# MLP entry of a two-layer hybrid step: twelve early weight pairs, earlier first splits, later squares and low parts

## The chip, the cores and the metric

The kernel runs on one core of one Trainium2 chip. The metric is device time in microseconds (us), here the median of three runs. The core has a matrix engine (PE), whose weight loads are a row of their own (PEld), a vector engine (DVE), a scalar engine (ACT), GpSimd (POOL), and a queue on SyncE (SP) that issues all DMA transfers in order.

## The reference, cut to what matters

Two layers. Each normalises the 1152 tokens (1024 latent, 128 prompt), runs three parallel groups (convolution, grouped attention, neighbourhood attention), adds their output projection, and then runs the MLP:

```
x = x + g1 * (concat(a_out, b_out, c_out) @ w_out)
h = rms(x, n2) * (1 + sc2) + sh2
x = x + g2 * (square(relu(h @ w1)) @ w2)
```

`w1` is 1024 x 4096, all in float32. The change touches only the step from the output projection through `h @ w1`.

## The kernel before

**Precision.** Each float32 product is made of three matmul passes (`three`, L1315): high part times high part, high times low, low times high. Each operand is split: ACT casts the high part (`w1h`, `HA`, `hi`), DVE subtracts it to get the low part (`w1l`, `low`). DVE works in the order written, ACT too; all orders are written by hand.

**Seven products for eight.** `h @ w1` goes by a Strassen-Winograd scheme over two halves of the model dimension, two halves of the tokens (576 each; T half 0 and 1), and pairs of weight columns. There are 16 pairs `g`; each needs seven products P1 to P7 (table `PRODUCTS`). One product is 24 matmuls of 288 columns. P1 and P2 need only the blocks B11 and B21, that is `h` of token half 0. The other five need sums in which half 1 takes part (blocks T1 to T4, B22).

**Early pairs.** So P1 and P2 of the first `EARLY` pairs are computed while the normalised half 1 is still being made. Their P1 result is stored to DRAM (`sd`) and read back (`again`) when the pair's other five products come; the weights A11 and A12 are loaded a second time with the pair's four blocks. I call this stretch the entry: it begins when PE ends the output projection (tile `pso`) and ends with the first P6 (tile `psb`). After it come five products for each early pair and seven for each later (late) pair.

**What runs in the entry.** The loop at L1665 goes over `seq`: three P1, then P2 and P1 in turn, three P2 at the end (`LEAD` 3). At each product it loads one weight block (`load_next`) and splits one (`begin_next`) that PE uses three products later; it computes the product (`psa` for P1, `psd` for P2) and takes the result out (`taken`: ACT copies P1 into `ev`; DVE adds P2 to it, and ACT then applies relu and square, `squared`). Then `next(pre)` runs one step of `norm2(L, 1)`: three steps of 1/rms, then per block index a step A that scales and shifts `X` (DVE, then ACT) and a step B that forms the sums of the halves (five DVE instructions and one ACT cast), then eight steps that cast the blocks and write their low parts (`low`). An extra step runs after every fourth product. A low part is held back by one call (`late`), so that DVE does not wait for the ACT cast just issued.

**Before the entry.** `out_proj` (L1321) makes eight output parts for each token half. During the last four parts of half 1 it runs `norm2(L, 0)` for half 0, and after each of them one step of `M.begin()`, whose eight steps are five loads and then three splits; the four steps left run behind the last part.

**After the entry.** For the late pairs of layer 0 every fourth product runs one step of `modulation(1, [0])` (`fill`): eight of its steps load four blocks `aw` of 256 KB each and do four matmuls. PSUM banks (`P`, eight) and the tiles of the shared pools S (18 of 2 x 576, among them `X`, `ev`, `low`) and T (18, among them all weight tiles) are given in turn.

Of the kernel before, what the change touches and what calls it, by code (L numbers as in the profile page):

```python
# [28 lines left out]
SEGS = [(0, 512), (512, 512), (1024, 128), (1024, 64), (1088, 64)]  # L29
HT, HH = 576, 288  # L30
ARENA = 229344 - 64 * NT
EARLY, LEAD = 8, 3
POOL_TAPS = 22
GPOOL = 6
SCAN = 12
# [10 lines left out]
def hybrid_step(ctx, tc, I, O, depth=DEPTH):  # L46
# [77 lines left out]
    sd = [dram.tile([EARLY, 128, 2 * HT], F32, name=f"sd{l}") for l in range(depth)]  # L124
    hd = [dram.tile([7, 16, 128, HT], F32, name=f"hd{l}") for l in range(depth)]
# [1195 lines left out]
    def out_proj(L, op, M):  # L1321
        l = L.l
        g1 = mod[l][:, :, 16:24]
        norms = {si: Norm(si, (nc.vector, nc.vector)) for si in (0, 3, 1, 4)}
        w, late = op.w, []

        def keep():
            while late:
                n, t = late.pop(0)
                load(dy[l][:, n, t * HT:(t + 1) * HT], X[n][:, t, :])  # L1330

        def part(n, t):
            ps = [P("pso"), P("pso")]
            for k in range(KT):
                three(ps, w[n][0][:, k, :], w[n][1][:, k, :], c_block(0, k, t), c_block(1, k, t), k == 0, k == KT - 1)
                yield "begun"
            update(ps, X[n][:, t, :], g1, n)
            norms[t].add(n)
            norms[3 + t].add(n)
            keep()  # L1340
            late.append((n, t))
            if t:
                w.pop(n)

        for n in range(KT):
            op.prep(n)
            if n == 0:
                yield from part(n, 0)
            op.prep(n + 1)
            if n:  # L1350
                run(part(n, 0))
            op.fetch()
            if n < 4:
                run(part(n, 1))
        keep()
        g0 = norm2(L, 0, norms)
        begin = M.begin()
        for n in range(4, KT):
            for k, _ in enumerate(part(n, 1)):
                if k in (1, 4, 6):  # L1360
                    next(g0, None)
            next(begin, None)
        run(begin)
        run(g0)
        yield "rest"
        for i, _ in enumerate(norm2(L, 1, norms)):
            if i == 2:
                keep()
            yield
# [18 lines left out]
    def norm2(L, t, norms):  # L1388

        l = L.l  # L1390
        gs = [norms[si].rstd() for si in (t, 3 + t)]
        for _ in range(3):
            for g in gs:
                next(g, None)
            yield

        def modulated(k):
            for s, si in enumerate((t, 3 + t)):
                x = xs(k, si)
                stt(x, x, A2[l][:, s, k:k + 1], norms[si].rstd_all, ALU.mult, ALU.mult)  # L1400
            for s, si in enumerate((t, 3 + t)):
                x = xs(k, si)
                act(x, x, ACTF.Identity, bias=mod[l][:, s, 24 + k:25 + k])

        late = []

        def parts(b, i, src):

            hi, lo = block(L, b, i)
            acopy(hi, src)  # L1410
            if late:
                late.pop()()
            late.append(partial(tt, lo, src, f32(hi), ALU.subtract))

        if t == 0:
            for i in range(4):
                for b, k in (("B11", i), ("B21", 4 + i)):
                    modulated(k)
                    parts(b, i, X[k][:, 0, :])
                    yield  # L1420
            late.pop()()
            return
        L.hi34 = {b: [S([2, HT], F32R, n="hi34") for _ in range(2)] for b in ("T3", "T4")}
        modulated(0)
        modulated(4)
        for i in range(4):
            if i < 3:
                modulated(i + 1)
                modulated(5 + i)
                yield  # L1430
            x1, x2, y1, y2 = X[i][:, 0, :], X[i][:, 1, :], X[4 + i][:, 0, :], X[4 + i][:, 1, :]
            raw = ha(10, i, HF)
            tt(x1, x2, x1, ALU.subtract)
            tt(raw, y2, x1, ALU.subtract)
            parts("T2", i, raw)
            tt(x2, y2, x2, ALU.subtract)
            tt(y1, y1, raw, ALU.subtract)
            yield
        L.low = {}
        for k in range(KT):  # L1440
            L.low[k] = S([2, HT], F32R, n="low")
            for u, b in enumerate(("T1", "T3") if k < 4 else ("T4", "B22")):
                parts(b, k % 4, X[k][:, u, :])
            yield
        late.pop()()


    class Mlp:
# [57 lines left out]
    def mlp(L, M, pre, fill, last):  # L1506
        l = L.l
        g2 = mod[l][:, :, 40:48]
        banks, ev, stores = {}, {}, []

        def keep(n=0):
            while len(stores) > n:
                load(*stores.pop(0))
# [90 lines left out]
        def squared(x):  # L1604
            act(x, x, ACTF.Relu)
            act(x, x, ACTF.Square)

        def taken(g, p, ps):
            early = g < EARLY
            if p == "P1":  # L1610
                ev[g] = [S([2, HT], n="ev")]
            if p == "P6":
                ev[g].append(S([2, HT], n="ev"))
            e1 = ev[g][0]
            e2 = ev[g][1] if len(ev[g]) > 1 else e1
            s1, h11 = e1[:, 0, :], e1[:, 1 if early else 0, :]
            u2, u3 = (e2[:, 0, :], e2[:, 1, :]) if early else (e1[:, 1, :], e2[:, 0, :])
            h21 = s1 if early else e2[:, 1, :]
            for h in range(2):
                c = slice(h * HH, (h + 1) * HH)  # L1620
                x = ps[h][:, 0:HH]
                to = {"P1": s1, "P2": h11, "P6": u2, "P5": u3, "P7": u3, "P3": u2, "P4": h21}[p][:, c]
                if p in ("P1", "P5") or p == "P6" and not early:
                    acopy(to, x)
                elif p == "P4" and not early:
                    act(to, x, ACTF.Relu)
                    tt(to, x, to, ALU.mult)
                else:
                    tt(to, x, (s1[:, c] if p in ("P2", "P6") else to), ALU.add)
            if p == "P2":  # L1630
                squared(h11)
                if early:
                    stores.append((sd[l][g], e1.rearrange("p a c -> p (a c)")))
                stores.append((hd[l][0, g], h11))
                if early:
                    del ev[g]
            elif p == "P7":
                if early:
                    tt(u3, u3, s1, ALU.add)
                squared(u3)  # L1640
                stores.append((hd[l][2, g], u3))
            elif p == "P3":
                squared(u2)
            elif p == "P4":
                if early:
                    squared(h21)
                stores.append((hd[l][1, g], h21))
                e3, e4 = S([2, HT], n="ev"), S([2, HT], n="ev")
                for b, o, x, y in ((3, e3[:, 0, :], u2, h11), (4, e3[:, 1, :], u3, e3[:, 0, :]),
                                   (5, e4[:, 0, :], u3, u2), (6, e4[:, 1, :], h21, e3[:, 1, :])):  # L1650
                    tt(o, x, y, ALU.subtract)
                    stores.append((hd[l][b, g], o))
                del ev[g]
# [10 lines left out]
            seq += [(g, "P2")] + [(g + LEAD, "P1")] * (g + LEAD < EARLY)  # L1664
        for x, (g, p) in enumerate(seq):  # L1665
            M.begin_next()
            product(g, p)
            keep(2)
            next(pre, None)
            if x % 4 == 3:  # L1670
                next(pre, None)
            if x == len(seq) - 6:
                M.load1(0, ("A11", "A21", "A22", "A12"))
            if x == len(seq) - 2:
                M.sums1(0)
        keep()
        again(0)
        seq = [(g, p) for g in range(EARLY) for p in ("P6", "P5", "P7", "P3", "P4")]
# [18 lines left out]
        for x, (g, p) in enumerate(seq):  # L1697
            if p == "P5" and g + 1 < NG:
                M.load1(g + 1, ("A11", "A21", "A22", "A12"))
            if p == "P7" and g + 1 < EARLY:  # L1700
                again(g + 1)
            prepare(x + 1)
            prepare(x + 2)
            product(g, p)
            keep(3)
            if g >= EARLY and x % 4 == 0:
                next(fill, None)
            if g == NG - 1 and p != "P1":
                for j in {"P2": (0, 1, 2, 3), "P6": (4, 5, 6, 7), "P5": (8, 9, 10, 11), "P7": (12, 13, 14, 15)}.get(p, ()):
                    load2("A12" if j < 8 else "A11", 0, j % 8)  # L1710
                if p in ("P6", "P5"):
                    fetch({"P6": 0, "P5": 2}[p])
# [260 lines left out]
```

## Time and profile before

| | |
|---|---|
| three runs | 3017.33, 3017.64, 3021.18 us, median 3017.64 |
| profiled execution, its time | 3022.51 us |
| its span, first to last instruction | 3020.7 us |
| granted PE clock, mean | 0.972 |
| PE busy | 2857.6 us (95%) |
| DVE, ACT, POOL busy | 2085.0, 1403.4, 650.5 us |

A timeline row reads: start, duration, engine, source line, instruction, output tile <- input tiles, shape, count, and in brackets the idle time just before and the instruction that ended it. Rows of equal instructions that follow each other are merged. A windows row gives for each stretch the busy time (and instructions) of each engine, the granted PE clock (1.00 is 2.4 GHz, 0.50 is 1.2 GHz), the busy share of the DMA engines and GB/s.

### The profile page before, as it was taken

The page shows a single profiled execution, that of the slowest core. Times are in us where ns is not written, and L with a number is a line of the kernel's source. Part 1 is how long each engine was busy: PE and PEld are TensorE (multiplying, and loading weights), DVE is VectorE, ACT ScalarE, POOL GpSimd, SP SyncE. Part 2 cuts the span into 40 slices and gives each one's busy share as a digit, 9 for nine tenths or more (in the row PEclk, how much of TensorE's full clock was granted, in tenths as well). Part 3 has the DMA queues.
Part 4 walks back from the last instruction along what each step waited for, and adds up shares of the span by engine and source line. Part 5 has one row for each costly group of instructions (what it writes and reads, how often), then busy time and mean ns, then how long its engine had stood idle before and what let it go on. Part 6 is the DMA issues. An engine that isn't in the chain of part 4 may idle for free.

```text
span 3020.7 us, 52765 instructions
## 1 busy us (share of the span) xinstructions
PE 2857.6 (95%) x20328; PEld 2540.2 (84%) x20328; DVE 2085.0 (69%) x3985; ACT 1403.4 (46%) x2880; POOL 650.5 (22%) x607
## 2 busy tenths in 40 slices
PE   6998999999889999999889999999997999999999
PEld 3878745799789999999878886458997999999999
DVE  6587778864767556758665877778557775585676
ACT  4334356763644444433452343568435444434344
POOL 3576345410000000000225762463100000000000
PEclk7999999999999999999989999999998999999999
DMA  7276302423466658443433671024334654575334
GB/s 282 82 209 172 97 24 55 101 81 114 134 197 200 207 165 297 162 154 95 139 122 98 186 205 59 16 59 105 95 119 155 194 174 158 174 253 175 126 96 164
DMA packets 424124, 430.42 MB, mean 142 GB/s; under 512 B 120000, under 2 KB 299968, under 8 KB 423872
## 3 DMA queue, kind: packets, MB, share of 16 engines
q1 hardware_dynamic: 423872, 427.04, 45.4%
q8 instruction: 160, 2.62, 0.4%
q14 instruction: 92, 0.75, 0.1%
HBM read 298.50 MB, written 128.45 MB: 141 GB/s over the span
## 4 chain that ended last, share of the span: by engine, by line
PE 74%; DVE 14%; ACT 4%; DMA 2%; issue 2%; POOL 2%; SPq 1%; DVEq 0%; POOLq 0%; ACTq 0%
PE ps L1319 23%; PE psa L1319 8%; PE psc L1319 7%; PE pso L1319 5%; PE psb L1319 5%; PE psacc L1118 3%; PE pspv L985 2%; DVE cacc L102 2%; PE psd L1319 2%; PE pspt L969 2%; PE psst L1132 2%; PE psm L1044 2%; PE pst L541 1%; PE pst L542 1%; PE pst L543 1%
## 5 line engine op out<-in xcount | busy, mean ns | idle before, releaser
L1319 PE MATMUL ps<-ts,w2h 128*128 128x288 f32 x3072 | 534.4, 296 | 8.3 <-DVE ts L99 4.8
L1319 PEld LDWEIGHTS ps<-ts,w2h 128*128 128x128 f32 x3072 | 451.7, 189 | 9.2 <-DVE ts L99 5.3
L1319 PE MATMUL ps<-ts,w2l 128*128 128x288 f32 x1536 | 329.2, 295 | 0.1
L96 ACT CAST ts<-ti 128x576 fp32r<-128x576 f32 x256 | 172.1, 672 | 314.4 <-PE ps L1319 216.4
L541 PE MATMUL pst<-wh,HA 128*128 128x256 f32 x1040 | 298.8, 287 | 0.0
L542 PE MATMUL pst<-wl,HA 128*128 128x256 f32 x1040 | 295.8, 284 | 0.0
L543 PE MATMUL pst<-wh,HA 128*128 128x256 f32 x1040 | 294.7, 283 | 0.0
L93 ACT ACTIVATE ev<-ev 128x576 f32<-128x576 f32 x224 | 153.7, 686 | 275.0 <-DVE ev L99 271.4
L1319 PEld LDWEIGHTS ps<-ts,w2l 128*128 128x128 f32 x1536 | 247.4, 189 | 0.4 <-DVE w2l L99 0.3
L99 DVE TENSOR_TENSOR ts<-ti,ts 128x576 fp32r<-128x576 f32 x256 | 194.6, 760 | 48.4 <-ACT ts L96 47.6
L102 DVE SCALAR_TENSOR_TENSOR X<-ps,mod,X 128x288 f32<-128x288 f32 x336 | 112.1, 408 | 161.4 <-PE ps L1319 161.4
L541 PEld LDWEIGHTS pst<-wh,HA 128*128 128x128 f32 x1040 | 199.6, 192 | 19.8 <-issue 7.6
L542 PEld LDWEIGHTS pst<-wl,HA 128*128 128x128 f32 x1040 | 199.3, 192 | 0.1
L543 PEld LDWEIGHTS pst<-wh,HA 128*128 128x128 f32 x1040 | 199.3, 192 | 0.0
L99 POOL TENSOR_TENSOR nacc<-nacc,nsq 128x512 f32<-128x512 f32 (+1 forms) x12 | 15.9, 1322 | 836.4 <-PE ps L1319 810.4
L1762 POOL COPY yu<-X 128x128 f32<-128x128 f32 x8 | 3.9, 499 | 855.2 <-DVE X L102 843.2
L99 DVE TENSOR_TENSOR w1l<-w1r,w1h 128x512 fp32r<-128x512 f32 x128 | 87.7, 689 | 133.6 <-ACT w1h L96 130.2
L1319 PE MATMUL pso<-HA,woh 128*128 128x288 f32 x1024 | 177.6, 295 | 0.0
L1046 DVE TENSOR_REDUCE mx<-psm 128x1 f32<-128x384 f32 x288 | 142.2, 546 | 31.9 <-PE psm L1044 31.7
L93 ACT ACTIVATE pt<-psst 128x512 f32<-128x512 f32 x216 | 118.2, 597 | 90.9 <-PE psst L1133 89.9
L99 POOL TENSOR_TENSOR R<-R,pt 128x1024 f32<-128x1024 f32 x60 | 148.3, 2472 | 27.9 <-ACT pt L93 25.9
L1319 PEld LDWEIGHTS pso<-HA,woh 128*128 128x128 f32 x1024 | 149.6, 188 | 0.0
(279 smaller groups left out, 7290.2 us busy)
## 6 DMA issues: line engine op xcount, KB each, us to landing
ti<-hd SPq DMA_DIRECT2D x128, 576.0 KB, 4.0
hd<-ev SPq DMA_DIRECT2D x224, 288.0 KB, 3.8
aw<-in_ada_w SPq DMA_DIRECT2D x160, 256.0 KB, 3.8
w1r<-in_mlp_w SPq DMA_DIRECT2D x160, 256.0 KB, 4.4
HF<-in_mlp_w SPq DMA_DIRECT2D x128, 256.0 KB, 5.1
ddA<-o SPq DMA_DIRECT2D x144, 128.0 KB, 2.9
wr<-in_w_in SPq DMA_DIRECT2D x28, 512.0 KB, 4.0
qd<-ddA SPq DMA_DIRECT2D x48, 256.0 KB, 3.3
```

Of the source, the lines that this page charges most:

```text
L93: nc.scalar.activation(out=out, in_=in_, func=func, scale=scale, bias=bias, **k)
L96: nc.scalar.copy(out, in_)
L99: (eng or nc.vector).tensor_tensor(out=out, in0=a, in1=b, op=op)
L102: nc.vector.scalar_tensor_tensor(out=out, in0=a, scalar=s, in1=b, op0=op0, op1=op1)
L541: mm(o, hi, wh, start=(k == 0), stop=False)
L542: mm(o, hi, wl, start=False, stop=False)
L543: mm(o, lo, wh, start=False, stop=(k == KT - 1))
L969: nc.tensor.transpose(ps[0:n, c], self.p[j][:, o:o + n], ident)
L985: mm(ps[64 * j:64 * j + 64, 0:128], v[j], self.at[j, i], start=(i == 0), stop=(i == nb - 1))
L1046: nc.vector.tensor_reduce(out=mx[j][:, qt, b:b + 1], in_=ps[:, 0:384], op=ALU.max, axis=AX.X)
L1118: mm(acc[64 * j:64 * j + 64, :], v, pt[:, j, :], start=(kt == 0), stop=(kt == 8))
L1319: mm(ps[h][:, 0:HH], x, y[:, h * HH:(h + 1) * HH], start=(start and z == 0), stop=(stop and z == 2), skip_group_check=True)
```

## The change

`EARLY` goes from 8 to 12. In the output projection two steps of `M.begin()` run ahead of each of the last four parts, where one ran behind it. Low parts are held back by two calls instead of one. The squares of an early pair and their stores are held until just before the next product, behind that product's weight split. The extra `norm2` step after every fourth product goes away. For the late pairs the `fill` step comes at every second product (there are 28 such products now, 56 before; 14 steps either way).

```
-EARLY, LEAD = 8, 3
+EARLY, LEAD = 12, 3
...
         for n in range(4, KT):
+            next(begin, None)
+            next(begin, None)
             for k, _ in enumerate(part(n, 1)):
                 if k in (1, 4, 6):
                     next(g0, None)
-            next(begin, None)
...
             acopy(hi, src)
-            if late:
-                late.pop()()
+            if len(late) == 2:
+                late.pop(0)()
             late.append(partial(tt, lo, src, f32(hi), ALU.subtract))
...
             if p == "P2":
-                squared(h11)
                 if early:
-                    stores.append((sd[l][g], e1.rearrange("p a c -> p (a c)")))
-                stores.append((hd[l][0, g], h11))
-                if early:
+                    def square():
+                        squared(h11)
+                        stores.append((sd[l][g], e1.rearrange("p a c -> p (a c)")))
+                        stores.append((hd[l][0, g], h11))
+
+                    held.append(square)
                     del ev[g]
+                else:
+                    squared(h11)
+                    stores.append((hd[l][0, g], h11))
...
             M.begin_next()
+            while held:
+                held.pop()()
             product(g, p)
             keep(2)
             next(pre, None)
-            if x % 4 == 3:
-                next(pre, None)
...
-            if g >= EARLY and x % 4 == 0:
+            if g >= EARLY and x % 2 == 0:
                 next(fill, None)
```

The order on ACT at the last part of the output projection in layer 0 (`nsq` are squares for the 1/rms of half 1, `w1h` the high parts of the first weight blocks, `psa` the first product), before:

```order
L96 CAST HA_68<-X_7685 128x576
L93 ACTIVATE X_8135<-X_8135,mod_101 128x512
L93 ACTIVATE X_8135<-X_8135,mod_101 128x64
L96 CAST HA_72<-X_8135 128x576
L93 ACTIVATE nsq_8570<-X_8135 128x512
L93 ACTIVATE nsq_8573<-X_8135 128x64
L96 CAST w1h_8583<-w1r_8343 128x512
L96 CAST w1h_8589<-w1r_8422 128x512
L96 CAST w1h_8595<-w1r_8502 128x512
L96 CAST w1h_8601<-w1r_8577 128x512
L96 COPY ev_8631<-psa_8605 128x288
```

and with the change:

```order
L96 CAST w1h_8515<-w1r_8266 128x512
L96 CAST w1h_8521<-w1r_8347 128x512
L93 ACTIVATE X_7685<-X_7685,mod_101 128x512
L93 ACTIVATE X_7685<-X_7685,mod_101 128x64
L96 CAST HA_68<-X_7685 128x576
L93 ACTIVATE X_8135<-X_8135,mod_101 128x512
L93 ACTIVATE X_8135<-X_8135,mod_101 128x64
L96 CAST HA_72<-X_8135 128x576
L93 ACTIVATE nsq_8592<-X_8135 128x512
L93 ACTIVATE nsq_8595<-X_8135 128x64
L96 CAST w1h_8601<-w1r_8349 128x512
L96 COPY ev_8631<-psa_8605 128x288
```

The first three weight casts (the first stands still earlier) no longer follow the last `nsq` pair; only the fourth does.

The order on DVE at the end of the entry in layer 0 (`psd` are P2 results, `w1S` the weight sums of pair 0, `w1l<-w1S` the low part of the first P6's weights), before:

```order
L99 TENSOR_TENSOR low_9207<-X_8067,HA_80 128x576
L99 TENSOR_TENSOR low_9244<-X_8135,hi_8764 128x576
L99 TENSOR_TENSOR w1S_9249<-w1r_9085,w1r_9087 128x512
L99 TENSOR_TENSOR w1S_9250<-w1S_9249,w1r_9083 128x512
L99 TENSOR_TENSOR w1r_9085<-w1r_9083,w1r_9085 128x512
L99 TENSOR_TENSOR w1S_9251<-w1r_9089,w1S_9250 128x512
L99 TENSOR_TENSOR ev_9167<-psd_9256,ev_9167 128x288
L99 TENSOR_TENSOR ev_9167<-psd_9257,ev_9167 128x288
L99 TENSOR_TENSOR low_9244<-X_8135,HA_80 128x576
L99 TENSOR_TENSOR w1l_9295<-w1S_9250,w1h_9293 128x512
```

and with the change:

```order
L99 TENSOR_TENSOR low_9357<-X_8135,HA_80 128x576
L99 TENSOR_TENSOR w1l_9411<-w1r_9200,w1h_9409 128x512
L99 TENSOR_TENSOR ev_9234<-psd_9413,ev_9234 128x288
L99 TENSOR_TENSOR ev_9234<-psd_9414,ev_9234 128x288
L99 TENSOR_TENSOR w1l_9443<-w1r_9244,w1h_9441 128x512
L99 TENSOR_TENSOR ev_9315<-psd_9478,ev_9315 128x288
L99 TENSOR_TENSOR ev_9315<-psd_9479,ev_9315 128x288
L99 TENSOR_TENSOR ev_9394<-psd_9508,ev_9394 128x288
L99 TENSOR_TENSOR ev_9394<-psd_9509,ev_9394 128x288
L99 TENSOR_TENSOR w1S_9538<-w1r_9403,w1r_9405 128x512
L99 TENSOR_TENSOR w1S_9539<-w1S_9538,w1r_9401 128x512
L99 TENSOR_TENSOR w1r_9403<-w1r_9401,w1r_9403 128x512
```

The last low part now stands ahead of the last four P2 results (the last of them, and the `w1l` of the first P6, follow right behind these rows); before, low parts stood between the last P2 results, the weight sums and that `w1l`.

The order on ACT behind the first P2 (`ev_8631` is pair 0's result, `x2` relu and square; `X` are the shifts of step A), as one piece of the difference:

```order
-L96 CAST w1h_8727<-w1r_8587 128x512
-L93 ACTIVATE ev_8631<-ev_8631 128x576 x2
+L96 CAST w1h_8727<-w1r_8513 128x512
 L93 ACTIVATE X_7319<-X_7319,mod_101 128x512
 L93 ACTIVATE X_7319<-X_7319,mod_101 128x64
```

```order
 L93 ACTIVATE X_7939<-X_7939,mod_101 128x64
+L96 CAST w1h_8781<-w1r_8519 128x512
+L93 ACTIVATE ev_8631<-ev_8631 128x576 x2
+L96 COPY ev_8813<-psa_8787 128x288
+L96 COPY ev_8813<-psa_8788 128x288
 L96 CAST HA_75<-HF_93 128x576
```

The squares moved behind step A and behind the next weight cast.

## Rows read from the trace of the kernel before

**Rows 1.** The page, busy time of each engine over the span.
```profile
PE 2857.6 (95%) x20328; PEld 2540.2 (84%) x20328; DVE 2085.0 (69%) x3985; ACT 1403.4 (46%) x2880; POOL 650.5 (22%) x607
```

**Rows 2.** Waits of PE over the whole span, those of the entries' tiles and of the modulation: who waited for whom, us in total, times, longest.
```profile
PE psb L1319 <- ACT w1h L96: 19.7, 2, 10.0
PE psa L1319 <- ACT w1h L96: 11.8, 2, 6.0
PE psmod L224 <- DMA aw<-in_ada_w: 9.1, 9, 1.9
PE psd L1319 <- ACT w1h L96: 7.9, 2, 4.0
PE psd L1319 <- DVE w1l L99: 4.2, 4, 1.4
```

**Rows 3.** Timeline of PE, layer 0: the end of the output projection, two products' starts in the middle, the first matmul after each long idle.
```profile
758.92 0.42 PE L1319 MATMUL pso<-HA,wol 128*128 128x288 f32 x2
765.30 1.33 PE L1319 MATMUL psa<-HA,w1h 128*128 128x288 f32 x4 [5.95 <-ACT w1h L96]
...
790.00 0.69 PE L1319 MATMUL psd<-HA,w1h 128*128 128x288 f32 x4
793.17 0.69 PE L1319 MATMUL psa<-HA,w1h 128*128 128x288 f32 x4
...
808.35 0.80 PE L1319 MATMUL psd<-HA,w1h 128*128 128x288 f32 x4 [3.96 <-ACT w1h L96]
...
838.58 1.33 PE L1319 MATMUL psb<-HA,w1h 128*128 128x288 f32 x4 [9.97 <-ACT w1h L96]
```

**Rows 4.** Timeline of PE, layer 1: the same last matmuls of the projection and the same first P6.
```profile
2253.11 0.43 PE L1319 MATMUL pso<-HA,wol 128*128 128x288 f32 x2
...
2333.11 1.33 PE L1319 MATMUL psb<-HA,w1h 128*128 128x288 f32 x4 [9.75 <-ACT w1h L96]
```

**Rows 5.** Windows of layer 0's entry, PE alone: stretch, its length, PE busy and matmuls, granted clock, DMA share, GB/s.
```profile
765.30:768.30 3.00, 3.00 (x13) 0.51 0.09 27
...
786.00:792.00 6.00, 6.00 (x48) 1.00 0.32 92
...
811.30:814.30 3.00, 3.00 (x14) 0.50 0.00 0
814.30:817.30 3.00, 3.00 (x18) 0.72 0.61 243
...
840.00:842.00 2.00, 2.00 (x10) 0.50 0.99 313
842.00:845.00 3.00, 3.00 (x20) 0.78 1.06 306
```

**Rows 6.** Timeline of DVE, layer 0: the last update of the output projection and the sum of squares of half 1 that follows; a step A; a weight split behind an ACT cast; a P2 result; one of the sums of step B; the first P6 result, which needs the P1 read back.
```profile
763.06 1.06 DVE L102 SCALAR_TENSOR_TENSOR X<-pso,mod,X 128x288 f32<-128x288 f32 x3
...
767.78 0.82 DVE L99 TENSOR_TENSOR nacc<-nacc,nacc 128x512 f32<-128x512 f32 x2
...
788.21 1.80 DVE L102 SCALAR_TENSOR_TENSOR X<-X,A,rstd 128x512 f32<-128x512 f32 x4
791.36 0.69 DVE L99 TENSOR_TENSOR w1l<-w1r,w1h 128x512 fp32r<-128x512 f32 x1 [1.34 <-ACT w1h L96]
791.97 0.81 DVE L99 TENSOR_TENSOR ev<-psd,ev 128x288 f32<-128x288 f32 x2
792.70 0.74 DVE L99 TENSOR_TENSOR X<-X 128x576 f32<-128x576 f32 x1
...
845.17 0.82 DVE L99 TENSOR_TENSOR ev<-psb,ev 128x288 f32<-128x288 f32 x2 [4.71 <-DMA ev<-sd]
```

**Rows 7.** Timeline of ACT, layer 0: the first weight casts, and the last squares with the casts for the first P6.
```profile
764.64 2.17 ACT L96 CAST w1h<-w1r 128x512 fp32r<-128x512 f32 x4
...
836.62 1.40 ACT L93 ACTIVATE ev<-ev 128x576 f32<-128x576 f32 x2 [3.52 <-DVE ev L99]
837.92 1.12 ACT L96 CAST w1h<-w1S 128x512 fp32r<-128x512 f32 x2
```

**Rows 8.** Timeline of ACT, layer 1: the copy of the P5 result, one per pair: the second and the eighth (last) early pair, the second and the eighth (last) late pair.
```profile
2357.84 0.70 ACT L96 COPY ev<-psc 128x288 f32<-128x288 f32 x2 [1.36 <-PE psc L1319]
...
2455.51 0.70 ACT L96 COPY ev<-psc 128x288 f32<-128x288 f32 x2 [1.38 <-PE psc L1319]
...
2500.84 0.70 ACT L96 COPY ev<-psc 128x288 f32<-128x288 f32 x2 [1.94 <-PE psc L1319]
...
2634.20 0.70 ACT L96 COPY ev<-psc 128x288 f32<-128x288 f32 x2 [1.94 <-PE psc L1319]
```

**Rows 9.** Windows by stage: layer 0's entry without its first three products, its early pairs, its late pairs. Busy time of PE, PEld, DVE, ACT, POOL, clock, DMA share, GB/s.
```profile
777.00:838.60 61.60, 45.45 (x317) 44.13 (x315) 49.52 (x90) 39.28 (x76) 0.00 (x0) 0.90 0.39 136
...
838.60:964.60 126.00, 125.88 (x915) 123.64 (x916) 89.76 (x162) 54.68 (x97) 0.00 (x0) 0.98 0.64 203
964.60:1153.00 188.40, 188.40 (x1422) 180.19 (x1421) 106.63 (x193) 84.90 (x169) 0.00 (x0) 1.00 0.59 195
```

**Rows 10.** DMA issues, 838.6 to 964.6 us (early pairs, first two rows) and 964.6 to 1096 us (late pairs with the modulation, last two): out <- in, count, KB each, median us to landing.
```profile
w1r<-in_mlp_w SPq DMA_DIRECT2D x32, 256.0 KB, 4.5
ev<-sd SPq DMA_DIRECT2D x8, 576.0 KB, 6.6
...
aw<-in_ada_w SPq DMA_DIRECT2D x32, 256.0 KB, 3.8
w1r<-in_mlp_w SPq DMA_DIRECT2D x23, 256.0 KB, 5.1
```

**Rows 11.** Windows of PE just after an idle of 2.55 us that ended at 89.22 us, and after one of 3.17 us that ended at 363.57 us: as in Rows 5.
```profile
89.22:91.22 2.00, 2.00 (x5) 0.50 0.01 4
91.22:93.22 2.00, 2.00 (x8) 0.71 0.00 0
...
363.57:365.57 2.00, 2.00 (x6) 1.00 0.00 0
```

More of the change, by code (lines that the diff above doesn't have):

```diff
@@ L1420, in norm2 @@
                     yield
-            late.pop()()
+            for x in late:
+                x()
             return
@@ L1444, in norm2 @@
             yield
-        late.pop()()
+        for x in late:
+            x()
     class Mlp:
@@ L1508, in mlp @@
         g2 = mod[l][:, :, 40:48]
-        banks, ev, stores = {}, {}, []
+        banks, ev, stores, held = {}, {}, [], []
         def keep(n=0):
@@ L1675, in mlp @@
                 M.sums1(0)
+        while held:
+            held.pop()()
         keep()
```

## The prediction, made before the change was run

> **What bounds the kernel now.** I read the page's busy shares first: PE is busy 95% of the span, DVE 69%, ACT 46% [rows 1]. So time can only come from stretches where PE stands still or runs at half clock. The list of who made PE wait comes second [rows 2]: the longest entries are the tiles `psb`, `psa` and `psd` waiting for the weight casts `w1h` and low parts `w1l`, 19.7 + 11.8 + 7.9 + 4.2 = 43.6 us in two layers. All of it lies in the two entries. The timeline of PE shows where [rows 3]: after the output projection ends (758.92 + 0.42 = 759.3) PE idles 5.95 us, then 3.96 us in the middle, then 9.97 us before the first P6 at 838.58; the short waits for `w1l` (4.2 us in four times, so 2.1 per entry) complete it. Layer 1 repeats it with 9.75 us at the end [rows 4]. Last I read the granted clock [rows 5]: after each of these idles PE runs at 1.2 GHz for some microseconds.
>
> One entry is thus 838.58 - 759.3 = 79.2 us for 16 products. A product at full clock takes 793.17 - 790.00 = 3.17 us [rows 3], 24 matmuls; 16 take 50.7. Idle is 5.95 + 3.96 + 9.97 + 2.1 = 22.0. Half clock inside the entry costs, by clock shares, 3.00 x 0.49 + 3.00 x 0.50 + 3.00 x 0.28 = 3.8 [rows 5]. That leaves 2.7 us for the 1/rms matmuls and small gaps; I keep it as it is.
>
> **Why PE idles.** At the start: DVE ran its last update of the projection only at 763.06, 3.7 us behind PE, ACT squared that result, and only then came the first weight casts at 764.64 [rows 6, 7]. At the end: the last squares ran at 836.62, because DVE's P2 result was queued behind low parts and weight sums, and the cast that P6 needs came behind them at 837.92 [rows 7]. In the middle DVE is the slow one.
>
> **The change, part by part, for one layer.**
>
> *Eight more products in the entry:* 8 x 3.17 = +25.4 us.
>
> *Four late pairs become early ones.* An early pair's period behind the entry is (2455.51 - 2357.84) / 6 = 16.28 us, a late pair's (2634.20 - 2500.84) / 6 = 22.23 [rows 8]. So 4 x 5.95 = -23.8 us. Two products are worth 6.34 us, so an early pair is dearer by 0.4 us: moving work alone costs 25.4 - 23.8 = +1.6 us. The pairs' extra DVE and ACT work (adding the P1 read back, more squares) is in that period already; DVE is busy 90 of 126 us there, ACT 55, and PE does not idle [rows 9].
>
> *First splits ahead of the last parts.* Three of the four casts leave the place behind the last squares, so the 5.95 us wait ends. Late next is DVE: the low part of B11's last block stands right before the update that began at 763.06. DVE now has three `w1l` (0.69 each) more in front of it and two waits on an ACT cast fewer, so I leave that time at about 763. The first P1 starts at 759.4 and needs that block at its last quarter, 2.6 us later: a wait of about 1 us. Behind the second P1 the 1/rms matmul needs the sum of squares, which was done at 767.78 + 0.82 [rows 6] and is now three `w1l` earlier relative to the update: about 767; PE is there at 766.7. I take 1.7 us for both. Bounds: nothing, and the 5.95 us.
>
> *Middle, with the extra norm step gone and low parts and squares later.* A round of two products is 6.34 us for PE. DVE needs a step A 1.80, a step B 5 x 0.70, two `w1l` 1.38, one P2 result 0.81, and 1.34 us in which it waits for a weight cast [rows 6]: 8.8. It falls back 2.5 us per round. Four rounds and a first step A of twice the size make 11.8; the splits run three products ahead, 9.5; DVE starts about 1 us behind. So PE waits 11.8 + 1 - 9.5 = 3.3 us in all, in pieces. Bounds: nothing (if the later squares and low parts end the 1.34 us waits), and the 3.96 + 2.1 us of before. The held squares pass one cast on ACT, and their stores go out one product later on SP; the weight loads queued behind them there run five products ahead of their cast, some 15 us, so I count nothing.
>
> *End of the entry.* After the last step B a product costs DVE two low parts (0.75 each), one `w1l` and half a P2 result, 2.6 us against PE's 3.17, so it has caught up well before the 24th product. What stays is a chain that nothing hides: P2 result 0.81, squares 1.40, cast 0.56 [rows 6, 7], and three handovers of 0.1: 3.1 us instead of 9.97. Bounds: this chain, and 9.97.
>
> *P1 read back for the first P6.* It landed at 845.17, 7.1 us after the squares ended (836.62 + 1.40). From the end of the last P2 that is now 0.81 + 1.40 + 0.2 + 7.1 = 9.5 us, and P7, which needs DVE to have read `psb`, comes 3.1 + 6.3 us after it, later with any half clock. At most 0.7 us; I count none beside the half clock.
>
> *Half clock.* Inside the entry 3.8 us go. Behind the first P6 it cost 2.00 x 0.50 + 3.00 x 0.22 [rows 5] and 0.64 in its first four matmuls (1.33 against 0.69 us) [rows 3]: 2.3 us. An idle of 2.55 us was followed by 2.00 x 0.50 + 2.00 x 0.29 = 1.6 us lost, one of 3.17 us by none [rows 11]. I take 1.6, so 3.8 + 2.3 - 1.6 = 4.5 us are gained.
>
> *Modulation twice as dense (layer 0).* Eight loads of 1 MB now come every 6.3 us instead of 12.7; 1.05 MB / 12.7 us = 83 GB/s more on top of 195 [rows 9], so 278, while 306 to 313 were moved at a share of 1 [rows 5]. It fits: zero. Its matmuls remain. The weight loads landed within 5.1 us in that stretch [rows 10], and PE needs them four products, 12.7 us, after their issue. The Trainium skill's page "DMA: Bandwidth & Descriptors" (Issuing engines are not separate DMA queues) says that all transfers interleave on the same 16 engines; by that rule the weight loads would slow down when the `aw` loads thicken, and the sum would lose what the DMA rival below names.
>
> **Sum per layer:** +25.4 - 23.8 - (22.0 - 1.7 - 3.3 - 3.1) - 4.5 = -16.8 us; both layers -33.6. On the profiled execution (3022.5 us, span 3020.7) that is 2989; it was 4.9 us above the median of the runs, so the median becomes 3017.6 - 33.6 = **2984.0 us**. One measurement can tell about 0.2%, 6 us, from no change.
>
> **Rivals.**
> *The lag reaches the end.* DVE does not catch up, because low parts wait for the stores of `ev` tiles whose place they take, and the 9.97 us wait stays: 6.9 us per layer and 0.7 of half clock, 2984 + 15 = 2999. For it: DVE was busy 49.5 of the last 61.6 us [rows 9]. Against it: the change spreads the same norm work over 24 products. Chance 0.12.
> *The waits all but vanish.* The 5.0 us of start and middle and the 1.6 of half clock go: 2984 - 13 = 2971. Chance 0.13.
> *DMA is the limit.* A pair more costs 2 x 576 KB for P1 out and back and 512 KB for A11 and A12 again; eight pairs 13.6 MB, at 313 GB/s 43.5 us if nothing were hidden: 3027. By 341 GB/s, which the same page gives for 1 MB transfers (Bandwidth), an estimate of 40 us. Against it: early pairs ran at share 0.64 without a wait of PE [rows 9]. Likelier is that the eight denser modulation loads make PE wait 1 us each, as `psmod` did elsewhere (9.1 us in nine times) [rows 2]: 2992. Chance 0.08 for both.
> *Slower: the entry keeps its pace per product.* If the hand-over between DVE and ACT at every product, and not the fixed norm work, sets the pace, 24 products take 24 x 79.2 / 16 = 118.8 us, +39.6 - 23.8 = +15.8 per layer: 3017.6 + 31.6 = 3049. It decides from 103.0 / 24 = 4.29 us per product upward. Against it: PE ran six microseconds at full clock without a gap in the middle of the norm steps [rows 5]. Chance 0.06.
>
> **How the numbers follow.** My forecast, 2974 to 2992, has 0.61. The range 2967 to 3000 adds the first two rivals and leaves out most of the DMA case and the slower one. Faster by over 0.2%: 0.61 + 0.12 + 0.13 and most of the DMA case, less a little for a cause that I do not see: 0.90. Within 0.2%: 0.04. Slower: 0.06.
>
> **What the profile after would show.** The entry at about 87 us with 24 products; PE's idle before the first `psa` near 1 us, in the middle under 4, before the first `psb` near 3; early pairs still 16.3 us apart, twelve of them. An idle before `psb` near 10 us, early pairs over 17 us apart, or waits of `psmod` or of weight sums on DMA in layer 0's late pairs would prove me wrong at that step.

## The result, and the profile after

The changed kernel takes 2984.14 us (median of 4, 2982.5 to 2987.05) beside 3019.41 for the kernel before; the ratio is 0.9882, interval 0.9865 to 0.9899. The forecast was 2984.0. The profiled execution took 2982.7 us, span 2980.9; all rows of "after" are from it.

The page's busy line answers to [rows 1], and the waits of PE over the whole span (who waited for whom, us, times, longest) to [rows 2]:

```profile
PE 2844.0 (95%) x20328; PEld 2525.2 (85%) x20328; DVE 2096.1 (70%) x4009; ACT 1401.0 (47%) x2864; POOL 652.5 (22%) x607
...
PE psmod L224 <- DMA aw<-in_ada_w: 10.7, 9, 1.7
...
PE psb L1319 <- ACT w1h L96: 5.6, 2, 2.8
PE psb L1319 <- DVE ev L99: 2.7, 3, 1.7
PE psa L1319 <- DVE HA L99: 2.3, 4, 0.8
PE psd L1319 <- DVE w1l L99: 1.2, 2, 0.6
PE psn L277 <- DVE nacc L99: 1.1, 2, 0.6
PE psd L1319 <- ACT w1h L96: 1.0, 2, 0.5
```

The work of PE is the same, 20328 matmuls. The 43.6 us of waits for weight casts and low parts are down to 8.2 (5.6 + 1.2 + 1.0 + 0.4 on `psa`, not shown). New are `psa` and `psn` waiting for DVE at the entry's start (2.3 and 1.1) and `psb` waiting for DVE's `ev` (2.7).

PE's timeline in layer 0's entry, all idles over 0.15 us, against [rows 3]; then the end of layer 1's, against [rows 4]:

```profile
759.19 0.54 PE L1319 MATMUL psa<-HA,w1h 128*128 128x288 f32 x2 [0.34 <-DVE HA L99]
...
761.38 0.53 PE L1319 MATMUL psa<-HA,w1h 128*128 128x288 f32 x2 [0.83 <-DVE HA L99]
...
765.90 1.29 PE L277 MATMUL psn<-nacc,ones 128*128 128x512 f32 x4 [0.55 <-DVE nacc L99]
...
799.70 0.54 PE L1319 MATMUL psa<-HA,w1l 128*128 128x288 f32 x2 [0.19 <-DVE w1l L99]
...
803.12 0.80 PE L1319 MATMUL psd<-HA,w1h 128*128 128x288 f32 x4 [0.51 <-ACT w1h L96]
...
804.50 0.53 PE L1319 MATMUL psd<-HA,w1l 128*128 128x288 f32 x2 [0.59 <-DVE w1l L99]
...
841.95 0.79 PE L1319 MATMUL psb<-HA,w1h 128*128 128x288 f32 x4 [2.81 <-ACT w1h L96]
...
2317.56 0.80 PE L1319 MATMUL psb<-HA,w1h 128*128 128x288 f32 x4 [2.81 <-ACT w1h L96]
```

The projection ends at 757.00 and the first `psa` follows without a wait. The entry, from there to the first `psb`, is 84.95 us for 24 products (79.24 for 16 before); 84.93 in layer 1. The windows of the entries (columns as in [rows 9]) show full clock throughout, where [rows 5] had stretches at half:

```profile
756.84:841.95 85.11, 79.27 (x582) 76.91 (x580) 66.67 (x125) 59.05 (x119) 0.00 (x0) 1.00 0.54 181
2232.46:2317.56 85.10, 79.28 (x582) 76.93 (x580) 66.66 (x125) 59.06 (x119) 0.00 (x0) 1.00 0.54 181
```

ACT's copies of the P5 result, the clock of the pairs, against [rows 8]: three of layer 0, then the second and the twelfth early pair of layer 1.

```profile
929.89 0.70 ACT L96 COPY ev<-psc 128x288 f32<-128x288 f32 x2 [0.46 <-PE psc L1319]
...
947.64 0.69 ACT L96 COPY ev<-psc 128x288 f32<-128x288 f32 x2
...
966.88 0.70 ACT L96 COPY ev<-psc 128x288 f32<-128x288 f32 x2 [1.32 <-PE psc L1319]
...
2341.67 0.70 ACT L96 COPY ev<-psc 128x288 f32<-128x288 f32 x2 [1.34 <-PE psc L1319]
...
2504.93 0.70 ACT L96 COPY ev<-psc 128x288 f32<-128x288 f32 x2 [1.35 <-PE psc L1319]
```

Layer 1 keeps its pace, (2504.93 - 2341.67) / 10 = 16.33 us. In layer 0 two early pairs took 17.75 and 19.24 us. So the gain went like this, in us, with the start of the second weights' matmuls (first `ps`: 1159.98 and 2645.59 before, 1143.49 and 2605.53 after) as the end of the pairs:

| stretch | forecast per layer | layer 0 | layer 1 |
|---|---|---|---|
| entry (products, idles, clock inside) | +7.7 | +5.71 | +5.36 |
| first `psb` to first P5 copy | -0.7 | -1.94 | -0.60 |
| first to last P5 copy | -23.8 | -17.94 | -23.88 |
| last P5 copy to `ps` | 0 | +0.02 | -0.03 |
| sum | -16.8 | -14.15 | -19.15 |

The rest of the span's 39.8 us, 6.5, lies outside these stretches: 2.3 before the projection's end in layer 0, 4.4 from `ps` of layer 0 to the projection's end in layer 1 (1093.6 us before, 1089.1 after), less 0.2 at the end. In the kernels of the experiments the first stretch ended between 756.3 and 762.1 us (759.3 before, 757.0 after), and the second took 1087.0 to 1093.4. Both vary that much from one execution to the next, so no part of the 6.5 us is shown to come from the change.

### The profile page after: what moved, and what is told of

It is laid out like the page before. It is cut to its first block, busy times and chain, and to the rows that moved or that the text cites. A ratio compares the mean times of both kernels' runs of the same rounds, so it can differ in the third digit from the quotient of the medians.

```text
span 2980.9 us, 52857 instructions
## 1 busy us (share of the span) xinstructions
PE 2844.0 (95%) x20328; PEld 2525.2 (85%) x20328; DVE 2096.1 (70%) x4009; ACT 1401.0 (47%) x2864; POOL 652.5 (22%) x607
## 4 chain that ended last, share of the span: by engine, by line
PE 76%; DVE 13%; ACT 4%; issue 2%; DMA 2%; POOL 2%; SPq 1%; DVEq 0%; POOLq 0%; ACTq 0%
PE ps L1319 23%; PE psb L1319 8%; PE psc L1319 6%; PE pso L1319 5%; PE psa L1319 5%; PE psd L1319 3%; PE psacc L1118 3%; PE pspv L985 2%; DVE cacc L102 2%; PE pspt L969 2%; PE pst L541 2%; PE pst L542 2%; PE pst L543 2%; PE psst L1132 2%; PE psm L1044 2%
## 5 line engine op out<-in xcount | busy, mean ns | idle before, releaser
L93 ACT ACTIVATE ev<-ev 128x576 f32<-128x576 f32 x240 | 164.7, 686 | 265.1 <-DVE ev L99 261.3
L102 DVE SCALAR_TENSOR_TENSOR cacc<-cin,vecs,cacc 128x1167 f32<-128x1167 f32 x78 | 136.8, 1754 | 11.3 <-POOL cacc L570 10.1
```

The lines of the kernel that those rows point to most:

```text
L93: nc.scalar.activation(out=out, in_=in_, func=func, scale=scale, bias=bias, **k)
L102: nc.vector.scalar_tensor_tensor(out=out, in0=a, scalar=s, in1=b, op0=op0, op1=op1)
```

## The experiments

Each is told against the kernel before on the same chip, as a ratio with its 95% interval. Entries and waits are from its own trace.

**The pairs alone.**
```
-EARLY, LEAD = 8, 3          (kernel before)
+EARLY, LEAD = 12, 3
```


> The kernel before with twelve early pairs and nothing else changed. My theory (moving pairs costs 1.6 us a layer, and eight products without norm work let DVE catch up before the first P6): the wait before the first psa stays near 6 us and the one in the middle near 4 to 6, the wait before the first psb falls from 10 to about 3; entry about 97.7 us; per layer +1.6 - 6.9 = -5.3, in all about -10.6 us against the kernel before (ratio 0.9965). Rival, the end wait comes from the order of squares and casts alone: it stays at 10 us, +3.2 us in all (ratio 1.001). Rival, the pairs bring the whole gain: -30 us or more (ratio 0.990).

3013.6 us, 0.998 (0.9969 to 0.9991). The entries are 98.16 and 97.42 us:

```profile
763.31 1.33 PE L1319 MATMUL psa<-HA,w1h 128*128 128x288 f32 x4 [5.95 <-ACT w1h L96]
...
855.52 0.99 PE L1319 MATMUL psb<-HA,w1h 128*128 128x288 f32 x4 [2.80 <-ACT w1h L96]
```

Start and middle wait as before, the end wait is 2.80: eight products without norm work let DVE catch up, as my theory said. The gain is smaller than my 10.6 because I forgot one thing: with four late pairs and a modulation block at every fourth product, half the blocks are left over and run behind the pairs. From the last P5 copy of layer 0 to its first `ps` it takes 24.79 us there, 11.34 before. From the projection's end to `ps`, layer 1, which has no modulation in it, gains 6.8 us, and layer 0 loses 4.5.

**The order alone.** The changed kernel with
```
-EARLY, LEAD = 12, 3
+EARLY, LEAD = 8, 3
 ...
+            if x % 4 == 3:
+                next(pre, None)
 ...
-            if g >= EARLY and x % 2 == 0:
+            if g >= EARLY and x % 4 == 0:
```


> The changed kernel with eight early pairs, the norm's additional step at every fourth product and the modulation at every fourth product as before: only the new order (first splits ahead of the last parts, low parts held by two, squares one product later). My theory: the start wait falls from 5.95 to about 1.7 us and its half clock (1.5 us) goes, the end wait falls only from 10 to about 8, since sixteen products leave DVE no time to catch up; about -8 us a layer, -16 in all against the kernel before (ratio 0.9947). Rival, the order does all and DVE does not lag: end wait 3 us, -18 a layer, -36 in all (ratio 0.988). Rival, the waits of start and middle are only moved to the end: 0 (ratio 1.000).

2997.88 us, 0.9924 (0.9911 to 0.9936). Entries 67.71 and 67.58. The start waits of layer 0 are 1.72 in all as in the changed kernel; then:

```profile
805.68 1.33 PE L1319 MATMUL psd<-HA,w1h 128*128 128x288 f32 x4 [3.97 <-ACT w1h L96]
...
829.85 1.33 PE L1319 MATMUL psb<-HA,w1h 128*128 128x288 f32 x4 [4.91 <-ACT w1h L96]
```

The order gives 22 us, more than I expected, since the end wait falls to 4.9 and not to 8. It is between my theory and the rival: 2.1 us of DVE's lag are left at the end, beside the 2.8 of the chain, and 4.3 us of waits stay in the middle (layer 0). The four more pairs then add 17.3 us to the entry; from the first to the last P5 copy they take off 18.3 us in layer 0 and 25.5 in layer 1 (forecast 23.8). In the stretches of the table above the order alone gives 21.7 us, the pairs alone 2.2 and the whole change 33.3. It is more than the two together because the denser modulation belongs to it too, and because the waits of the middle need both the new order and a norm without its extra step: 4.3 us stay here with the first alone, 4.7 with the second alone (squares and low parts as before, below). No run takes the extra step back by itself.

**First splits behind the last parts.** The changed kernel with
```
-            next(begin, None)
-            next(begin, None)
             for k, _ in enumerate(part(n, 1)):
 ...
+            next(begin, None)
```


> The changed kernel with the loads and first three splits one step behind each of the last four parts, as in the kernel before. My theory: the wait before the first psa is back at about 6 us (+6 with 1.5 of half clock, less the 1.7 of the short waits that it covers), the 1.3 us in the middle may go; +4.5 us a layer, +9 in all against the changed kernel (about 0.991 of the kernel before). Rival, the wait is only moved, DVE uses it to catch up: +2 in all (0.989). Rival, the lag is carried on through the entry: +7.5 a layer, +15 (0.993).

2993.84 us, 0.9912 (0.9898 to 0.9926). The first `psa` waits 5.68 and 5.64 us, the middle keeps its 1.3, the entries are 89.97 and 90.60, so 5.0 and 5.7 longer. My theory holds for the place; that the middle's waits might go was wrong.

**Squares and low parts as before.** The changed kernel with
```
-            if len(late) == 2:
-                late.pop(0)()
+            if late:
+                late.pop()()
 ...
-            while held:
-                held.pop()()
             product(g, p)
+            while held:
+                held.pop()()
```


> The changed kernel with squares right after their product and low parts held by one, as in the kernel before. My theory: DVE waits for casts again (1.3 us in each round of two products while the norm's second part runs), PE's waits in the middle grow from 1.3 to about 5 us, the end chain stays at 2.8; +4 a layer, +8 in all against the changed kernel (0.991 of the kernel before). Rival, the holding does nothing once the norm work is spread over 24 products: 0 (0.988). Rival, the lag reaches the end: +10 a layer (0.995).

2994.79 us, 0.9915 (0.9901 to 0.9929); entries 90.99 and 90.97, +6.0. PE's idles in the middle of layer 0 are 4.7 us instead of 1.3:

```profile
796.37 0.54 PE L1319 MATMUL psa<-HA,w1l 128*128 128x288 f32 x2 [0.74 <-DVE w1l L99]
...
800.74 0.82 PE L1319 MATMUL psd<-HA,w1h 128*128 128x288 f32 x4 [1.46 <-ACT w1h L96]
...
805.54 0.54 PE L1319 MATMUL psa<-HA,w1l 128*128 128x288 f32 x2 [0.59 <-DVE w1l L99]
...
808.96 0.82 PE L1319 MATMUL psd<-HA,w1h 128*128 128x288 f32 x4 [0.50 <-ACT w1h L96]
...
811.17 0.53 PE L1319 MATMUL psd<-HA,w1l 128*128 128x288 f32 x2 [1.40 <-DVE w1l L99]
```

DVE's waits for the casts whose low parts it is to form, in the middle and the end of this entry (us, times, longest); the kernel before has the same three:

```profile
DVE low L99 <- ACT hi L96: 2.7, 2, 1.4
DVE low L99 <- ACT HA L96: 2.7, 2, 1.4
...
DVE HA L99 <- ACT HA L96: 1.5, 2, 0.7
```

They are 6.9 us, and in the same stretch of the changed kernel these three lines don't exist. But the four waits of `low` (5.4 us) lie between 815 and 837 us, behind PE's last wait in the middle. Ahead of it lie the two of `HA` (1.5 us) and DVE's waits for the weight cast, three in each kernel, which are longer here because squares stand ahead of that cast on ACT. Two of the three, in the changed kernel and then in this one:

```profile
786.99 0.69 DVE L99 TENSOR_TENSOR w1l<-w1r,w1h 128x512 fp32r<-128x512 f32 x1 [1.34 <-ACT w1h L96]
...
794.88 0.69 DVE L99 TENSOR_TENSOR w1l<-w1r,w1h 128x512 fp32r<-128x512 f32 x1 [1.34 <-ACT w1h L96]
```
```profile
782.19 0.69 DVE L99 TENSOR_TENSOR w1l<-w1r,w1h 128x512 fp32r<-128x512 f32 x1 [1.96 <-ACT w1h L96]
...
790.71 0.69 DVE L99 TENSOR_TENSOR w1l<-w1r,w1h 128x512 fp32r<-128x512 f32 x1 [1.97 <-ACT w1h L96]
```

Three times 0.6 and 1.5 add up to the 3.4 us by which PE's idles in the middle grew. Most of the rest of the 6.0 lies, in layer 0, in products of 3.3 to 3.5 us instead of 3.17 (1.9 us in all), and in layer 1 in half clock behind the last of these waits.

**Low parts alone as before** (the first of the two edits above).

> The changed kernel with low parts held by one instead of two; squares stay one product later. With both undone the entry took 91.0 us against 85.0. My theory: the low part that follows its cast at once makes DVE wait for ACT, and that is most of it; entry 89 us, +8 in all against the changed kernel (0.9905 of the kernel before). Rival, the squares are what counts, since they stand ahead of the next weight cast on ACT: entry 86 us, +2 (0.9885).

2988.2 us, 0.9898 (0.9881 to 0.9914); entries 87.55 and 87.67, +2.6 and +2.7, so neither theory: if the two parts add up, low parts make 2.6 of the six and squares 3.4. In this trace the two `low` lines are gone and the `HA` line is still there: the later squares ended the first, the later low parts the second.

**Modulation as sparse as before.** The changed kernel with
```
-            if g >= EARLY and x % 2 == 0:
+            if g >= EARLY and x % 4 == 0:
```


> The changed kernel with a block of the next layer's modulation at every fourth product of the late pairs instead of every second. In the kernel with twelve pairs alone, which does the same, 26.9 us lay between the last copy of a P5 result and the second weights' first matmul of layer 0, against 14.3 in the changed kernel, while its late pairs took 94.0 us against 100.0. My theory: half of the blocks are left over and wait for their loads there, +12.6 - 6.0 = +6.6 us against the changed kernel (0.990 of the kernel before). Rival, the wait there belongs to something else: the late pairs get shorter, -6 (0.986).

2987.77 us, 0.9891 (0.9876 to 0.9905). The late pairs of layer 0 take 94.0 us instead of 99.9, and the first `ps` comes 25.28 us behind the last P5 copy instead of 11.36. The changed kernel then waits 1.5 us longer for the second input of `ps`, so it is +6.5 us in that layer, as expected; in the ratio (0.9882 and 0.9879 for the changed kernel) the step lies within the intervals. Who waits there:

```profile
PE psmod L224 <- DMA aw<-in_ada_w: 6.6, 1, 6.6
```

**Ten pairs.** `EARLY, LEAD = 10, 3` in the changed kernel.

> The changed kernel with ten early pairs: 20 products for the 18 steps of the norm. My theory (a pair moved costs 0.4 us; from eight to twelve pairs only the time to catch up is gained): waits of start and middle stay at 1.7 and 1.3 us, the end at 2.8 to 4, four products fewer (-12.7) against two late pairs more (+11.9): -0.8 a layer, +1 if the end wait grows, so within 3 us of the changed kernel (0.987 to 0.989 of the kernel before). Rival, every pair more is worth 3 us as the step from eight to twelve seemed: +6 a layer, +12 (0.992).

2988.07 us, 0.9897 (0.9881 to 0.9913). Start and middle wait the same 1.72 and 1.29, but:

```profile
833.48 1.33 PE L1319 MATMUL psb<-HA,w1h 128*128 128x288 f32 x4 [4.73 <-ACT w1h L96]
```

1.9 us of lag are left at the end, +1.1 a layer by the sum. From the projection's end to `ps` the two layers together take 760.6 us, against 759.4 and 757.1 in two executions of the changed kernel. The medians differ by more, which the intervals don't resolve; the rival of 12 us is out.

**The changed kernel again**, unedited.

> The changed kernel once more, unedited. If the two long early pairs of layer 0 (17.8 and 19.2 us against 16.3) belong to the program, they stand at the same place again; if they are DMA jitter of one execution, they are elsewhere or gone. Half clock behind the 2.8 us idle before the first P6: none in the profile of after; by my theory of a drop that follows such an idle in some executions only, it may show here. Time 2984, ratio 0.988.

2981.75 us, 0.9879 (0.9863 to 0.9895). Layer 0's sixth to eighth P5 copies are 16.78 and 17.48 us apart: the slow pairs come back, smaller. The clock just behind the first `psb`, first of after, then of this one (layer 0 and 1 in each):

```profile
843.95:846.95 3.00, 3.00 (x25) 3.00 (x24) 0.00 (x0) 0.00 (x0) 0.00 (x0) 1.00 1.00 293
...
2319.56:2322.56 3.00, 3.00 (x15) 3.00 (x14) 0.00 (x0) 0.00 (x0) 0.00 (x0) 0.54 1.01 296
```
```profile
847.03:850.03 3.00, 3.00 (x15) 3.00 (x14) 0.00 (x0) 0.00 (x0) 0.00 (x0) 0.50 1.01 313
...
2322.33:2325.33 3.00, 3.00 (x25) 3.00 (x24) 0.00 (x0) 0.00 (x0) 0.00 (x0) 1.00 1.00 300
```

The same idle of 2.8 us is followed by 1.2 GHz in one layer and not in the other, and the layers change places. My expectation read none in the profile of after; its layer 1 has it.

**Weight loads a product earlier in the program.**
```
-            if p == "P5" and g + 1 < NG:
+            if p == ("P6" if g < EARLY else "P5") and g + 1 < NG:
 ...
-            if p == "P7" and g + 1 < EARLY:
+            if p == "P5" and g + 1 < EARLY:
```


> The changed kernel with the four weight loads of the next early pair issued one product earlier, and the read-back of P1 too. My theory (the early pairs of 17.8 and 19.2 us in layer 0 come from weights that landed 0.8 and 1.9 us after DVE wanted them): with 3.2 us more lead all early pairs are 16.3 us apart, -4 us in all against the changed kernel (0.987). Rival, DMA bursts with all stores, loads and read-backs of a pair at share 1 set the pace, and the wait moves to the read-back: 0 (0.988). Rival, earlier loads take the place of stores and buffers come free later: +4 (0.9895).

2985.53 us, 0.9887 (0.9869 to 0.9905). The slow pairs stay (four of 16.5 to 17.2 us), so the edit did not do what it was for. SP's queue tells why: the loads still went out at 896.90, 913.86 and 931.06, each right behind a row of stores that waits for DVE's and ACT's results. The program's order had moved, the issue had not.

**First cast and read-back early.** The changed kernel with the read-back and the split for the first P6 issued two products before the entry's end (`prepare` and its list of products move ahead of the loop for it, not shown):
```
             if x == len(seq) - 2:
                 M.sums1(0)
+                again(0)
+                prepare(0)
         while held:
             held.pop()()
         keep()
-        again(0)
```


> The changed kernel, but the read-back of the first pair's P1 and the weight cast and low part for the first P6 are issued before the last product of the entry instead of behind its squares. My theory (the 2.8 us before the first psb are P2 result, squares and cast in a row, and only the cast is needed): that wait falls to under 0.4 us, and DVE no longer waits for the read-back (4.1 and 3.5 us before); -2.5 a layer, -5 in all against the changed kernel (0.9865 of the kernel before). Rival, the cast only pushes the last P2 result and squares behind it, and a wait of the same size turns up before the first P7: 0 (0.988).

2973.75 us, 0.985 (0.9832 to 0.9868). Layer 0, ACT then PE:

```profile
838.93 0.62 ACT L96 CAST w1h<-w1S 128x512 fp32r<-128x512 f32 x1 [3.10 <-DVE w1S L99]
839.45 1.40 ACT L93 ACTIVATE ev<-ev 128x576 f32<-128x576 f32 x2
...
840.75 0.53 PE L1319 MATMUL psb<-HA,w1l 128*128 128x288 f32 x2 [0.22 <-DVE w1l L99]
```

The cast now stands before the last two pairs' squares (the second row has the first of them), the wait is 0.2 us, and no half clock follows. The entries are 82.0 us, 3.0 shorter, 6.0 in all. The medians differ from the changed kernel's two by 8.0 and 10.4 us, and from the projection's end to `ps` the two layers together take 749.5 us, 7.7 and 9.9 less than in those two executions. What the entries leave of it is half clock behind the first P6, and shorter early pairs in layer 0 against one of the two.

**And fewer stores ahead of the loads.** To the last kernel:
```
-            keep(3)
+            keep(5 if g < EARLY else 3)
```


> The kernel with the read-back and the first cast issued early, and with up to five instead of three stores held back while early pairs run, so that on SP the weight loads of the next pair no longer stand behind stores that wait for results. My theory (the weight loads land only just in time because SP issues them about 6.3 us ahead of their use; any slow burst then makes DVE wait): SP issues them some 6 us earlier, all early pairs in both layers are 16.3 us apart, -1.5 to -3 us against that kernel (0.984 to 0.9845 of the kernel before). Rival, the slow pairs come from all transfers of a pair together: early pairs of 17 us stay, 0 (0.985). Rival, later stores free the ev tiles later and the read-back waits: +4 (0.9865).

2973.74 us, 0.9847 (0.9832 to 0.9861). SP issues the four loads at 902.41, DVE uses them 14.4 us later; in the changed kernel it is 6.6 us in most pairs, and 8.6 with a wait in the slowest. Changed kernel first, then this one, each with SP's issue and DVE's first use:

```profile
929.27 2.40 SPq L144 DMA_DIRECT2D w1r<-in_mlp_w  x4
...
937.90 0.69 DVE L99 TENSOR_TENSOR w1S<-w1r,w1r 128x512 f32<-128x512 f32 x1 [1.94 <-DMA w1r<-in_mlp_w]
```
```profile
902.41 2.13 SPq L144 DMA_DIRECT2D w1r<-in_mlp_w  x4
...
916.77 0.68 DVE L99 TENSOR_TENSOR w1S<-w1r,w1r 128x512 f32<-128x512 f32 x1
```

Behind the first copy, all early pairs of both layers are 16.27 to 16.31 us apart but one (16.67), and DVE's wait for weights is gone but for 0.27 us in the first pair. In the median nothing is seen of it beside the kernel without it (slow pairs of 16.61 and 17.47). The runs of both kernels (2972.9 to 2978.3 us) lie below all of the changed kernel's (2981.4 to 2987.1).

## Why the prediction was right

*Start:* forecast 1.7 us, measured 0.34 + 0.83 + 0.55 = 1.72, by the two items named (low parts of B11, here of its last two blocks, and the sum of squares). The experiment with late splits puts 5.0 to 5.7 us a layer back.

*Middle:* forecast 3.3, measured 0.19 + 0.51 + 0.59 = 1.29. The step that failed is DVE's lag of 11.8 us. Its round was taken as 8.8 us; DVE's waiting weight splits stand 7.9 us apart in the changed kernel (779.09, 786.99 and 794.88). The wait of 1.34 us for the cast, which I thought might go, is still in each of them. What left the first two rounds is a low part, 0.7 us: held back by two calls, the first of them comes only in the third. I had counted five instructions for every step B, and priced the later low parts at nothing but a bound. The fourth round also has no step A (1.80 us in my sum): at 799.57 DVE adds a P2 result and at 800.30 it begins step B. With both put right the sum gives no wait at all, so the 1.3 us left are not explained by it. With squares and low parts as before PE idles 4.7 us there, and the entry is 6.0 us longer.

*End:* forecast 3.1, measured 2.81, and the chain (P2 result, squares, cast) is the cause. Here it is in layer 0 of the changed kernel, ahead of the `psb` at 841.95:

```profile
839.15 0.81 DVE L99 TENSOR_TENSOR ev<-psd,ev 128x288 f32<-128x288 f32 x2
...
840.00 1.40 ACT L93 ACTIVATE ev<-ev 128x576 f32<-128x576 f32 x2 [1.85 <-DVE ev L99]
841.30 1.12 ACT L96 CAST w1h<-w1S 128x512 fp32r<-128x512 f32 x2
```

Issuing the cast ahead of it ends the wait. That DVE catches up with 24 products and not with 16 is shown by ends of 4.9 (8 pairs, with the norm's extra step), 4.73 (10) and 2.81 (12), and by 2.80 with twelve pairs in the old order. So the rival "the lag reaches the end" is out, and with entries of 67.7, 74.2 and 85.0 us for 16, 20 and 24 products the slower one too.

*Half clock:* inside the entry as forecast, none left. Behind the first P6 I took 1.6 us; it is there in one layer of two, in either execution of the changed kernel, and costs 1.5 and 2.5 us (from the first `psb` to the first P5 copy 8.24 and 9.25 us, 6.71 where the clock stays full). The read-back, counted at nothing, kept DVE waiting (3.5 us in layer 1) but no wait of PE shows there.

*Pairs:* forecast -23.8, layer 1 -23.88. In layer 0 only -17.94: 4.4 us in two early pairs, 1.0 in the denser modulation (late pairs 11.0 us over the 22.23 of a plain one; eight of them 10.0 before). In the two slow pairs PE waits 0.89 and 1.67 us for DVE, and half clock behind the second wait costs another 1.7. I had read 16.28 us in layer 1 and no wait of PE in layer 0, and not that weights used 6.6 us after their issue have next to no slack: in the kernel before, the load that DVE's first sum waits for last landed only 0.1 to 1.2 us ahead of it. That kernel had the same order on SP and ran through at 16.3; only at its change from early to late pairs in layer 1 did DVE wait 1.15 us for weights. Every other trace here shows an early pair of 16.5 us or more, the one with eight pairs too (17.06 in layer 1). Issuing the loads 14 us ahead ends the wait in the one trace of it; what slows single transfers stays open. The load on the DMA engines alone doesn't tell the two apart: their share (the last but one number) from issue to use was no higher in the slowest pair than in one that came in time:

```profile
929.30:937.30 8.00, 7.11 (x53) 6.80 (x52) 4.57 (x9) 2.62 (x6) 0.00 (x0) 1.00 0.96 275
...
879.50:886.10 6.60, 6.58 (x49) 6.26 (x48) 4.59 (x9) 1.41 (x4) 0.00 (x0) 1.00 0.97 268
```

The mean share of 0.64, which I held against the rival of DMA, hides that the loads of every pair come in bursts near 1.

*DMA:* the modulation at every second product made PE wait for no `aw` in the late pairs (for 0.4 us in one of the experiments), and at every fourth it would have cost 6.5 us. I had added its loads up to 278 GB/s; the late pairs of layer 0 moved 241 (from 1032 to 1133 us), at a share of 0.73. The Trainium skill's page "DMA: Bandwidth & Descriptors" (Issuing engines are not separate DMA queues) has all transfers interleave on 16 engines; the trace agrees, the weight loads there landed in 6.2 us (median) instead of 5.1 [rows 10], and PE's lead covered it.

So the total is right partly by chance: the entries came out 2.0 to 2.3 us a layer better and the clock behind the first P6 1.2 in layer 0, layer 0's pairs 5.9 worse, and all this cancels within 1 us of the forecast's 33.6 (33.3 measured in the changed stretches). That the time is 2984.1 to the forecast's 2984.0 is luck beyond it: the medians lie 35.3 us apart, the profiled executions 39.8, by stretches that the change isn't shown to touch.

## What to carry to other kernels

When two engines hand results to each other at every step, let the consumer run one item later, and put work that nobody waits for behind the result that somebody does: here that ended 6.9 us of DVE's waits and shortened others, without removing an instruction. Only those ahead of PE's own waits shortened the middle, so look at where a wait lies before you count it. Look at what stands last in a stretch: here three short instructions in a row (2.8 us) stayed exposed however well the rest overlapped, and another order removed the wait. A load here went out only behind the stores in front of it on SP's queue, which waited for their results, whatever its place in the program; read its issue time in the queue's timeline.

## What was not expected of the hardware

An idle of PE of 2.80 to 2.81 us ahead of the first `psb` stands in 16 entries of eight traces here. Behind nine of them the granted clock fell to 0.50 within 1.5 us, behind seven it stayed at 1.00; in two executions of the changed kernel it was each layer once. Behind the 0.2 us of the last two kernels it stayed at 1.00 in all four entries. An idle of 1.67 us among the early pairs (949.18 in layer 0 of after) was followed by half clock as well. Four weight loads of 256 KB, issued together, served DVE's first sum only 8.6 us after their issue in one pair (929.27 to 937.90), 7.5 us in the pair before it, and 6.6 us in most others of the same stage, with a DMA share between 0.96 and 1.02 in each case.
